# Hybrid decoder on one core: the rotated key rows written once a layer into four lasting K tiles, and two query squares added before their sums

## The chip, the cores and the metric

The kernel runs on one core of a Trainium2 chip. The metric is device time in microseconds (us), the median over several runs of the whole program. The engines of a core are named as the profile names them: PE is TensorE (matmuls and transposes), PEld its weight load, DVE is VectorE, ACT is ScalarE, POOL is GpSimd, and SP is SyncE, which issues the DMA transfers here.

## The reference

512 tokens with 1024 features go through two layers and a last RMSNorm. All is float32. Cut to what matters here:

```python
n = rmsnorm(h)
p = n @ W_in                      # RWKV groups, latents of the MLA, two gate groups
y_A = rwkv7_time_mix(p_A) @ W_oA  # 8 heads x 64; a group norm per head at the end
y_B = mla(p_B) @ W_oB             # 8 heads
h = h + (sigmoid(g_A) * y_A + sigmoid(g_B) * y_B) @ W_out
h = h + conv_ffn(rmsnorm(h))

def mla(q_lat, kv_lat, k_pe):     # widths 256, 128, 32
    q = rmsnorm(q_lat) @ w_q_up   # per head 64 plain + 32 rotary columns
    kv = rmsnorm(kv_lat) @ w_kv_up
    k_pe = rope(k_pe)             # one rotary key, the same for all 8 heads
    s = (q_nope @ k_nope + q_pe @ k_pe) * scale, causal
    return softmax(s) @ v
```

Two facts of it bear on the change: the rotated key rows are the same for all heads of a layer, and the RMSNorm of the query latent needs the sum of squares over 256 features, which the kernel holds as two tiles of 128 features.

## The kernel before

Tiles are 128 partitions x 512, features on the partitions and tokens along the row. A big matmul is done three times (L247 hi x hi, L248 lo x hi, L249 hi x lo), since each operand is split in two parts of lower precision. Weights come in units of 512 KB by DMA into `raw`; ACT makes the upper part `whi` (L202), DVE the lower part `wlo` (L203); there are two buffers of each. These matmuls are most of the program.

The stage around the change is the mixer of each layer. It runs in these steps.

1. **Inversion.** For the time mix, triangular 32x32 blocks are inverted on DVE: 30 dependent pairs of a product `tm` (L663) and an addition into `X` (L665), then the transposes `T11` (L667) and `T22` (L669), which the matmuls at L750 read. Meanwhile PE works on the weight units of the three latents (`lat`, two for q and one for kv, L689) and of the rotary key. The order of PE is written out by hand here (`tc.manual_schedule`). For each latent ACT makes the squares `lsq` (L693). `lsum` adds them over the features with `tok_sums` (L326): a matmul with one output column for each block of 128 tokens and each tile of squares, so 8 for the two query latents and 4 for the kv latent. DVE scales the sum (`nv`, L305), POOL takes the power -1/2 (L306), ACT spreads it (`nw`), and PE's transposes with a DVE step give `rq` (L319) and `rk`. Between them DVE computes the rotated key rows `kp` in three steps (L728 to L730) into the lower half (rows 64 to 127) of a tile. After that, DVE scales the kv latent (L736).
2. **Scan** over eight chunks, also in PE order by hand. POOL scales the state there (`tmp`, L815).
3. **Outputs, norms, heads.** `chunk_out` writes the output Y of the time mix into `Z`. `group_norm` and `group_scale` norm it for four blocks of tokens: DVE reduces (L856 to L860), POOL takes the power (L862) and scales (`Z`, L867). PE transposes the four normed blocks (L873, `xy<-cst,Z`). Beside this run the attention heads in four pairs, `heads(0)` to `heads(3)`. A pair has its plain key rows from PE, which ACT copies into K[0:64]; POOL copies `kp` into K[64:128] (L918); `q` is written by DVE (L925). Then come the scores `sc` (L933), the softmax in `P` on DVE (L936, L940) and ACT (L939, L941), the transposes `pt` (L944), their copies `PT` (L946) and the product `po` (L953), with the PE order by hand for L953 alone.

Outside of the parts ordered by hand a list scheduler sets the order of each engine when the program is built; it uses its own estimates of durations and the free buffers of each pool. K and q share five buffers (tag `qk`).

Of the kernel before, what the change touches and what calls it, by code (L numbers as in the profile page):

```python
# [9 lines left out]
F32 = mybir.dt.float32  # L10
# [3 lines left out]
ALU = mybir.AluOpType  # L14
# [144 lines left out]
def build(ctx, tc, x, pos, wst, vecd, constd, out):  # L159
    nc = tc.nc  # L160
    V, A, G, PE = nc.vector, nc.scalar, nc.gpsimd, nc.tensor

    def pool(**kw):
        return tc.tile_pool(reuse_waits="tile", **kw)
# [107 lines left out]
    def acc():  # L272
        return accp[-1].tile([128, 512], F32, name="acc", tag="acc")
# [19 lines left out]
    def rsqrt_tok(ps, n, eps, js=range(4), pool=sm, tag="nsq", bufs=1):  # L293

        v = rsqrt_col(ps, n, eps, js)
        w = pool.tile([128, 512], F32, name="nw", tag=tag, bufs=bufs)
        a, b = js[0], js[-1] + 1
        A.copy(w[:, 128 * a:128 * b].rearrange("p (j n) -> p j n", n=128),
               v[:, a:b, None].to_broadcast([128, b - a, 128]))
        return w  # L300
# [21 lines left out]
    def tok_sums(ps, sq, js=range(4)):  # L322
        sq = sq if isinstance(sq, list) else [sq]
        for j in js:
            for i, t in enumerate(sq):
                PE.matmul(ps[:, j:j + 1], t[:, 128 * j:128 * j + 128], ones[:, 0:1], start=i == 0, stop=i == len(sq) - 1)  # L326
# [100 lines left out]
    def mixer(l, ops, nrm, wks):  # L427
        with ExitStack() as mx:
# [209 lines left out]
            tl = mx.enter_context(pool(name=f"tl{l}", bufs=1))  # L638
# [3 lines left out]
            def sc(name="sc"):  # L642
                return pb.tile([128, 512], F32, name=name, tag="sc", bufs=2)
# [7 lines left out]
            with pool(name=f"ti{l}", bufs=2) as ti, tc.manual_schedule(engines={PE.engine}):  # L651
# [32 lines left out]
                lat, sq = [], []  # L684

                def lat_end(ps):
                    i = len(lat)
                    o = (tl if i < 3 else ti).tile([128, 512], F32, name=f"lat{i}", bufs=1)
                    V.tensor_tensor(o, ps, rstd, ALU.mult)  # L689
                    lat.append(o)  # L690
                    if i < 3:
                        sq.append(ti.tile([128, 512], F32, name="lsq", tag="lsq", bufs=3))
                        A.activation(sq[i], o, AF.Square)  # L693

                def a_ak_v(i):
                    ps = xyt()
                    for hd in range(8):
                        for e in range(2):
                            ur, vr = rows(e)
                            PE.matmul(ps[ur:ur + 64, e, 64 * hd:64 * hd + 64], AM[vr:vr + 64, hd, 2 * i + e, ur:ur + 64],  # L700
                                      Z[vr:vr + 64, i, e, 64 * hd:64 * hd + 64], start=True, stop=True, tile_position=(vr, ur))
                    for e in range(2):
                        ur, vr = rows(e)
                        A.copy(Z[ur:ur + 64, i, e, :], ps[ur:ur + 64, e, :])

                def lsum(i, t, n):
                    ssq = sc()
                    tok_sums(ssq, t)
                    return rsqrt_tok(ssq, n, NORM_EPS, pool=ti, tag="lsq", bufs=3)
# [9 lines left out]
                for i in range(3):  # L719
                    parts4[i].go()  # L720
                a_ak_v(0)
                w0 = lsum(0, sq[0:2], 256.0)
                parts4[3].go(4)
                w1 = lsum(1, sq[2], 128.0)
                parts4[3].go()
                kp = tl.tile([128, 512], F32, name="kp", bufs=1)
                k2 = ti.tile([128, 512], F32, name="k2", tag="lsq", bufs=3)
                V.tensor_tensor(kp[64:128, :], lat[3][0:64, :], tabs[0][0:64, :], ALU.mult)  # L728
                V.tensor_tensor(k2[64:128, :], lat[3][64:128, :], tabs[0][64:128, :], ALU.mult)
                V.tensor_tensor(kp[64:128, :], kp[64:128, :], k2[64:128, :], ALU.add)  # L730
                rq = tl.tile([128, 512], F32, name="rq", bufs=1)
                spread(w0, tabs[1], rq, sc)
                a_ak_v(1)
# [47 lines left out]
                for c in range(8):  # L781
                    i, e = divmod(c, 2)
# [38 lines left out]
            with pool(name=f"tb{l}", bufs=2) as tb:  # L821
                def MT(name, tag, bufs=3):
                    return tb.tile([128, 512], F32, name=name, tag=tag, bufs=bufs)
# [87 lines left out]
                def heads(p):  # L911
                    psk = acc()
                    mm3(psk, [w[:, 128 * p:128 * p + 128] for w in lk], kvop, True, True)
                    qs, ks = [], []
                    for hh in range(2):
                        K = MT("K", "qk", 5)
                        A.copy(K[0:64, :], psk[64 * hh:64 * hh + 64, :])
                        G.tensor_copy(K[64:128, :], kp[64:128, :])  # L918
                        ks.append(K)
                    for hh in range(2):  # L920
                        psq = acc()
                        for j in range(2):
                            mm3(psq, W.get(), qops[j], j == 0, j == 1)
                        q = MT("q", "qk", 5)
                        V.tensor_tensor(q, psq, rq, ALU.mult)  # L925
                        qs.append(q)
                    po = pb.tile([128, 512], F32, name="po", tag="po")
# [42 lines left out]
    for l in range(DEPTH):  # L970
# [7 lines left out]
        with pool(name=f"h{l + 1}", bufs=8, side="right") as hp, accs(f"accC{l}", 6):  # L978
# [31 lines left out]
            with pool(name=f"ff{l}", bufs=44) as fp:  # L1010
# [39 lines left out]
                if last:  # L1050
                    m = KT - 1
                    ws = [W.get() for _ in range(FT)]
                    with tc.manual_schedule(engines={PE.engine}):
                        for f in range(2):
# [10 lines left out]
                            sq = sm.tile([128, 512], F32, name="sq7", tag="nsq", bufs=1)  # L1065
# [47 lines left out]
```

## Time and profile before

| | |
|---|---|
| runs before | 1574.63 us median of 3 (1572.89 to 1576.72) |
| profiled execution, first to last instruction (span) | 1573.0 us |
| time around the span in the profiled execution | not given apart from the span; the runs' median is 1.6 us above it |
| instructions | 22441 |
| mean granted clock of PE over the span | 0.997 |
| L306, POOL power on 128x4 or 128x8, 10 times | 10.0 us in all, 998 ns each |
| L342, POOL addition of squares in the larger norms, 14 times | 25.0 us in all, 1787 ns each |
| L933, scores, 128 times | 44.4 us in all, 447 ns each |
| L203, DVE lower parts of weights, 249 times | 306.8 us in all, 1233 ns each |

The profile shows one execution. The busy time of an engine is the time in which its instructions run, with no register, branch or semaphore work. The chain of work is followed back from the last instruction: at each step to what released it. In the rows of the timeline the columns are start, duration, engine, line, operation, written tile and read tiles with their shapes; in brackets stand the idle time before the row and what ended it. Lines are those of the kernel before.

### The profile page before, as it was taken

The page shows a single profiled execution, that of the slowest core. Times are in us where ns is not written, and L with a number is a line of the kernel's source. Part 1 is how long each engine was busy: PE and PEld are TensorE (multiplying, and loading weights), DVE is VectorE, ACT ScalarE, POOL GpSimd, SP SyncE. Part 2 cuts the span into 40 slices and gives each one's busy share as a digit, 9 for nine tenths or more (in the row PEclk, how much of TensorE's full clock was granted, in tenths as well). Part 3 has the DMA queues.
Part 4 walks back from the last instruction along what each step waited for, and adds up shares of the span by engine and source line. Part 5 has one row for each costly group of instructions (what it writes and reads, how often), then busy time and mean ns, then how long its engine had stood idle before and what let it go on. Part 6 is the DMA issues. An engine that isn't in the chain of part 4 may idle for free.

```text
span 1573.0 us, 22441 instructions
## 1 busy us (share of the span) xinstructions
PE 1543.9 (98%) x9052; PEld 1248.4 (79%) x9052; DVE 917.0 (58%) x1476; ACT 664.0 (42%) x1004; POOL 184.4 (12%) x157
## 2 busy tenths in 40 slices
PE   8999999899999999999999999998999999999998
PEld 6887886678888888888878888776788888888887
DVE  6579786666555555533346768858574555554332
ACT  6445444663443333322244544447444433333222
POOL 1011102300310110100001110013002101100000
PEclk9999999999999999999999999999999999999999
DMA  6324322234323322233342333213353223222322
GB/s 207 115 94 144 118 82 68 82 94 148 121 94 95 102 98 94 94 113 119 110 147 93 109 107 121 75 49 103 100 168 101 94 95 104 97 94 94 102 99 81
DMA packets 57273, 166.09 MB, mean 106 GB/s; under 512 B 6352, under 2 KB 8528, under 8 KB 57168
## 3 DMA queue, kind: packets, MB, share of 16 engines
q1 hardware_dynamic: 57024, 164.48, 32.1%
q8 instruction: 71, 1.16, 0.3%
q14 instruction: 34, 0.28, 0.1%
q10 hardware_dynamic: 144, 0.16, 0.0%
HBM read 147.32 MB, written 17.30 MB: 105 GB/s over the span
## 4 chain that ended last, share of the span: by engine, by line
PE 90%; DVE 5%; ACT 2%; issue 1%; POOL 0%; DMA 0%; SPq 0%; POOLq 0%; DVEq 0%; ACTq 0%
PE acc L247 26%; PE acc L248 26%; PE acc L249 26%; PE sc L933 2%; PE pt L944 1%; PE po L953 1%; PE m L603 1%; PE xy L799 1%; DVE wlo L203 1%; PE m L611 1%; PE xy L808 0%; ACT whi L202 0%; DVE X L665 0%; DVE tm L663 0%; PE xy L789 0%
## 5 line engine op out<-in xcount | busy, mean ns | idle before, releaser
L247 PE MATMUL acc<-hi,whi 128*128 128x512 f32 (+1 forms) x1910 | 750.7, 393 | 6.0 <-ACT hi L283 5.1
L249 PE MATMUL acc<-hi,wlo 128*128 128x512 f32 (+1 forms) x1910 | 743.3, 389 | 1.7 <-issue 0.9
L248 PE MATMUL acc<-lo,whi 128*128 128x512 f32 (+1 forms) x1910 | 743.2, 389 | 0.0
L202 ACT CAST whi<-raw 128x1024 fp32r<-128x1024 f32 (+2 forms) x249 | 253.4, 1019 | 540.0 <-PE acc L248 466.6
L247 PEld LDWEIGHTS acc<-hi,whi 128*128 128x128 f32 x1910 | 359.6, 188 | 80.6 <-ACT hi L283 5.1
L249 PEld LDWEIGHTS acc<-hi,wlo 128*128 128x128 f32 x1910 | 359.5, 188 | 76.3 <-issue 1.7
L248 PEld LDWEIGHTS acc<-lo,whi 128*128 128x128 f32 x1910 | 359.8, 188 | 71.7 <-issue 0.8
L203 DVE TENSOR_TENSOR wlo<-raw,whi 128x1024 fp32r<-128x1024 f32 (+2 forms) x249 | 306.8, 1233 | 176.0 <-ACT whi L202 175.5
L1033 POOL TENSOR_TENSOR c<-c,rstd 128x512 f32<-128x512 f32 x44 | 58.0, 1317 | 403.5 <-ACT c L1032 403.5
L1026 DVE TENSOR_TENSOR u<-acc,rstd 128x512 f32<-128x512 f32 x44 | 30.5, 692 | 104.4 <-PE acc L249 104.3
L1035 DVE TENSOR_TENSOR c<-c,acc 128x512 f32<-128x512 f32 x44 | 30.3, 688 | 86.4 <-POOL c L1033 86.4
L1032 ACT ACTIVATE c<-c 128x512 f32<-128x512 f32 x44 | 27.8, 632 | 81.7 <-DVE c L1031 81.7
L306 POOL TENSOR_TENSOR nv<-nv,cst 128x4 f32<-128x4 f32 (+1 forms) x10 | 10.0, 998 | 337.2 <-DVE nv L305 335.9
L342 POOL TENSOR_TENSOR nacc<-nacc,nsq 128x512 f32<-128x512 f32 x14 | 25.0, 1787 | 193.7 <-ACT nsq L341 193.7
L933 PE MATMUL sc<-K,q 128*128 128x128 f32 (+3 forms) x128 | 44.4, 447 | 1.6 <-DVE q L925 1.6
L452 DVE TENSOR_TENSOR cur<-acc,rstd 128x512 f32<-128x512 f32 x28 | 19.1, 689 | 45.2 <-PE acc L249 37.7
L939 ACT ACTIVATE P<-P,mn 128x128 f32<-128x128 f32 (+3 forms) x64 | 35.5, 556 | 20.7 <-issue 9.3
L941 ACT ACTIVATE P<-P,mn 128x128 f32<-128x128 f32 (+3 forms) x64 | 34.4, 557 | 8.0 <-DVE mn L940 8.0
L1029 ACT ACTIVATE c<-u,vec 128x512 f32<-128x512 f32 x44 | 35.7, 811 | 2.8 <-DVE u L1025 2.8
L936 DVE CUSTOM_DVE_ANT_0 P<-sc,cst 128x128 f32<-128x128 f32 (+3 forms) x64 | 30.6, 483 | 5.9 <-PE xy L873 2.9
L1031 DVE SCALAR_TENSOR_TENSOR c<-u,vec,c 128x512 f32<-128x512 f32 x44 | 33.1, 752 | 1.5
L1030 DVE SCALAR_TENSOR_TENSOR c<-u,vec,c 128x512 f32<-128x512 f32 x44 | 32.8, 746 | 1.8 <-ACT c L1029 1.8
(247 smaller groups left out, 1356.7 us busy)
## 6 DMA issues: line engine op xcount, KB each, us to landing
raw<-in_w SPq DMA_DIRECT2D x238, 512.0 KB, 3.4
gate_d<-gg SPq DMA_DIRECT2D x32, 256.0 KB, 2.1
AM<-gate_d SPq DMA_DIRECT2D x16, 256.0 KB, 5.0
gb<-gate_d SPq DMA_DIRECT2D x16, 256.0 KB, 3.6
h<-in_x SPq DMA_DIRECT2D x8, 256.0 KB, 4.3
rgate_d<-gt SPq DMA_DIRECT2D x8, 256.0 KB, 2.6
bl_d<-rk SPq DMA_DIRECT2D x8, 256.0 KB, 4.4
bl<-bl_d SPq DMA_DIRECT2D x8, 256.0 KB, 2.6
```

Of the source, the lines that this page charges most:

```text
L202: A.copy(hi, r)
L203: V.tensor_tensor(lo, r, hi.bitcast(F32), ALU.subtract)
L247: PE.matmul(ps, w[0], xx[0], start=first, stop=False)
L248: PE.matmul(ps, w[0], xx[1], start=False, stop=False)
L249: PE.matmul(ps, w[1], xx[0], start=False, stop=last)
L933: PE.matmul(sp[:, 0:n], qs[hh][:, 128 * b:128 * b + 128], ks[hh][:, 0:n], start=True, stop=True)
L939: A.activation(P[:, 0:n], P[:, 0:n], AF.Exp, bias=mn[:, 0:1], scale=-1.0, accum_out=mn[:, 1:2])
L941: A.activation(P[:, 0:n], P[:, 0:n], AF.Copy, scale=mn[:, 2:3])
L1029: A.activation(cc, u[:, 2:514], AF.Identity, bias=vc(l, "conv_b", i), scale=vc(l, "conv_w", 2 * FT + i))
L1030: V.scalar_tensor_tensor(cc, u[:, 1:513], vc(l, "conv_w", FT + i), cc, ALU.mult, ALU.add)
L1031: V.scalar_tensor_tensor(cc, u[:, 0:512], vc(l, "conv_w", i), cc, ALU.mult, ALU.add)
L1033: G.tensor_tensor(cc, cc, rstd, ALU.mult)
```

## The change

Two parts. First, the squares of the two query latents are added on POOL into one tile as soon as both are there, so that `lsum(0, ...)` takes four one-column matmuls a layer in place of eight. Second, four tiles `K0` to `K3` of the mixer's lasting pool `tl` take the place of the eight K tiles of a layer's heads. DVE writes the rotated rows straight into `K0[64:128]`, POOL copies them into the other three right away, in the inversion, and `heads(p)` writes only rows 0 to 63 of the pair of tiles that is its turn (`K0`, `K1` for p = 0 and 2, `K2`, `K3` for p = 1 and 3). The q tiles have a tag of their own with three buffers. A layer has three POOL copies of the rotated rows in place of eight.

```diff
@@ lat_end(ps)
                         sq.append(ti.tile([128, 512], F32, name="lsq", tag="lsq", bufs=3))
                         A.activation(sq[i], o, AF.Square)
+                        if i == 1:
+                            G.tensor_tensor(sq[0], sq[0], sq[1], ALU.add)
...
                 a_ak_v(0)
-                w0 = lsum(0, sq[0:2], 256.0)
+                w0 = lsum(0, sq[0], 256.0)
                 parts4[3].go(4)
                 w1 = lsum(1, sq[2], 128.0)
                 parts4[3].go()
-                kp = tl.tile([128, 512], F32, name="kp", bufs=1)
+                Ks = [tl.tile([128, 512], F32, name=f"K{i}", bufs=1) for i in range(4)]
+                kp = Ks[0]
                 k2 = ti.tile([128, 512], F32, name="k2", tag="lsq", bufs=3)
                 V.tensor_tensor(kp[64:128, :], lat[3][0:64, :], tabs[0][0:64, :], ALU.mult)
                 V.tensor_tensor(k2[64:128, :], lat[3][64:128, :], tabs[0][64:128, :], ALU.mult)
                 V.tensor_tensor(kp[64:128, :], kp[64:128, :], k2[64:128, :], ALU.add)
+                for K in Ks[1:]:
+                    G.tensor_copy(K[64:128, :], kp[64:128, :])
                 rq = tl.tile([128, 512], F32, name="rq", bufs=1)
@@ heads(p)
-                    qs, ks = [], []
+                    qs, ks = [], Ks[2 * (p % 2):2 * (p % 2) + 2]
                     for hh in range(2):
-                        K = MT("K", "qk", 5)
-                        A.copy(K[0:64, :], psk[64 * hh:64 * hh + 64, :])
-                        G.tensor_copy(K[64:128, :], kp[64:128, :])
-                        ks.append(K)
+                        A.copy(ks[hh][0:64, :], psk[64 * hh:64 * hh + 64, :])
                     for hh in range(2):
                         psq = acc()
                         for j in range(2):
                             mm3(psq, W.get(), qops[j], j == 0, j == 1)
-                        q = MT("q", "qk", 5)
+                        q = MT("q", "q")
                         V.tensor_tensor(q, psq, rq, ALU.mult)
```

The lines behind the first added one move down by 2, those behind the key rows by 5, those behind the head's first loop by 2. Two places of the order that the scheduler and the program give show what moves.

POOL in layer 0, from ahead of the inversion through the scan to the first group norm, before (`whi` and `wlo` into `lk`: weights of the keys; `St`, `PC`: the scan's state and decay; `mu`: the group norm's statistics):

```order
L579 TENSOR_TENSOR BKb<-BK,z 128x1024
L306 TENSOR_TENSOR nv<-nv,cst 128x4 x2
L815 TENSOR_TENSOR tmp<-St,PC 128x256 x3
L901 CAST lk_2584<-whi 128x512
L901 CAST lk_2586<-wlo 128x512
L918 COPY K<-kp 64x512
L815 TENSOR_TENSOR tmp<-St,PC 128x256
L918 COPY K<-kp 64x512 x2
L815 TENSOR_TENSOR tmp<-St,PC 128x256 x2
L918 COPY K<-kp 64x512
L862 TENSOR_TENSOR mu<-mu,cst 128x8
```

The same stretch of POOL after:

```order
L579 TENSOR_TENSOR BKb<-BK,z 128x1024
L695 TENSOR_TENSOR lsq<-lsq 128x512
L306 TENSOR_TENSOR nv<-nv,cst 128x4 x2
L735 COPY K_1966<-K_1965 64x512
L735 COPY K_1967<-K_1965 64x512
L735 COPY K_1968<-K_1965 64x512
L820 TENSOR_TENSOR tmp<-St,PC 128x256 x3
L906 CAST lk_2587<-whi 128x512
L906 CAST lk_2589<-wlo 128x512
L820 TENSOR_TENSOR tmp<-St,PC 128x256 x3
L867 TENSOR_TENSOR mu<-mu,cst 128x8
```

An addition of 128x512 and three copies of 64x512 now stand in the inversion, where POOL had only the two small powers; the four copies during the scan are gone.

PE in layer 0, around the third of the group norm's transposes (`xy<-cst,Z`), before; `acc` are the queries of a later head:

```order
L933 MATMUL sc<-K,q 128x128
L247 MATMUL acc<-hi,lk_2584 128x512
L248 MATMUL acc<-lo,lk_2584 128x512
L873 MATMUL xy<-cst,Z 128x128 x2
L249 MATMUL acc<-hi,lk_2586 128x512
L933 MATMUL sc<-K,q 128x128
L247 MATMUL acc<-hi,whi 128x512
L933 MATMUL sc<-K,q 128x256
L873 MATMUL xy<-cst,Z 128x128
L248 MATMUL acc<-lo,whi 128x512
```

The same place of PE after:

```order
L935 MATMUL sc<-K_1967,q 128x128
L247 MATMUL acc<-hi,lk_2587 128x512
L248 MATMUL acc<-lo,lk_2587 128x512
L878 MATMUL xy<-cst,Z 128x128 x2
L249 MATMUL acc<-hi,lk_2589 128x512
L878 MATMUL xy<-cst,Z 128x128
L935 MATMUL sc<-K_1968,q 128x128
L247 MATMUL acc<-hi,whi 128x512
L935 MATMUL sc<-K_1967,q 128x256
L248 MATMUL acc<-lo,whi 128x512
```

The third transpose now stands ahead of a score, a weight matmul and a longer score that stood ahead of it; the fourth comes after the rest of the query's matmuls and a score of 384 columns, where before it came after two scores of 512. In layer 1 the same pieces move.

## The prediction

> **What bounds the kernel now.** The page comes first: the busy shares and the chain of work that ended last.
>
> ```profile
> span 1573.0 us, 22441 instructions
> PE 1543.9 (98%) x9052; PEld 1248.4 (79%) x9052; DVE 917.0 (58%) x1476; ACT 664.0 (42%) x1004; POOL 184.4 (12%) x157
> PE 90%; DVE 5%; ACT 2%; issue 1%; POOL 0%; DMA 0%; SPq 0%; POOLq 0%; DVEq 0%; ACTq 0%
> ```
>
> TensorE is busy for 98% and carries 90% of the chain, so a change counts only where TensorE idles, or by taking work from it while nothing else is late. Next comes the table of busy time by stretch (columns: stretch, length, then the busy time of PE, PEld, DVE, ACT and POOL, the granted clock, the DMA share, GB/s). The first row is the triangular inversion of layer 0, the two below it are the group norms of layers 0 and 1, and the last is the rest of layer 0's attention heads.
>
> ```profile
> 190.00:223.00 33.00, 33.00 (x268) 27.36 (x268) 30.64 (x77) 13.10 (x19) 2.26 (x2) 1.00 0.25 79
> 283.00:307.00 24.00, 19.95 (x271) 13.77 (x270) 17.05 (x48) 14.08 (x35) 12.61 (x11) 0.93 0.32 111
> 1060.00:1084.00 24.00, 20.08 (x280) 14.06 (x280) 18.18 (x52) 15.50 (x37) 12.61 (x11) 1.00 0.34 111
> 307.00:345.00 38.00, 37.80 (x259) 26.57 (x259) 28.41 (x84) 29.99 (x74) 0.61 (x1) 1.00 0.22 66
> ```
>
> Two places matter. In the inversion PE is busy all the time, but DVE is too (30.64 of 33.00 us; what is left are gaps of 0.03 between dependent steps, and two waits). In the group norms PE idles 4.05 and 3.92 us. Behind them it idles 0.20 us, so PE is the bound again there, and what is lost before stays lost.
>
> **The inversion: which engine ends last.** The timeline's columns are start, duration, engine, line, operation; in brackets the idle time before it and its releaser.
>
> ```profile
> 196.80 0.63 ACT L693 ACTIVATE lsq<-lat 128x512 f32<-128x512 f32 x1 [1.38 <-DVE lat L689]
> 200.96 1.95 PE L326 MATMUL sc<-cst,lsq 128*128 128x1 f32 x16
> 205.61 0.95 PE L326 MATMUL sc<-cst,lsq 128*128 128x1 f32 x8
> 205.58 0.41 DVE L665 TENSOR_TENSOR X<-X,tm 128x240 f32<-128x240 f32 x1
> 206.60 0.16 DVE L305 TENSOR_SCALAR nv<-sc 128x4 f32<-128x4 f32 x1 [0.61 <-PE sc L326]
> 209.44 0.69 DVE L689 TENSOR_TENSOR lat<-acc,rstd 128x512 f32<-128x512 f32 x1 [0.19 <-PE acc L249]
> 223.16 2.19 DVE L667 STREAM_TRANSPOSE T<-X 128x1024 f32<-128x1024 f32 x1
> 225.40 2.21 PE L750 MATMUL sc<-T,AM 32*32 32x32 f32 x128 [0.35 <-DVE T L667]
> ```
>
> DVE's chain of tm and X ends in the transpose T; PE stands waiting for it (0.35 us). So DVE sets the end of this stage.
>
> *The sums.* Four of eight one-column matmuls go (8 records of 16): 1.95 - 0.95 = 1.0 us of PE. PE comes 1.0 us earlier to a wait that DVE ends, so by itself this is worth nothing. What it does free is DVE's two waits on PE: 0.61 and 0.19, less the usual gap of 0.03 each, so 0.74 us a layer.
>
> *The added addition and the three copies* stand on POOL, which is empty there. The squares that the addition reads are there at 197.43, its sums begin at 200.96, and the copies were made at 254.0 us at the earliest before (last row below), so by their own duration they cost nothing. The question is what they do to DVE. No row has POOL at work beside the tm and X chain on tiles of this size; the nearest rows are these.
>
> ```profile
> 80.83 1.92 POOL L579 TENSOR_TENSOR BKb<-BK,z 128x1024 f32<-128x1024 f32 x1 [7.21 <-DVE BK L573]
> 80.73 0.69 DVE L588 TENSOR_TENSOR rk<-m,v 128x512 f32<-128x512 f32 x1
> 81.34 2.48 DVE L203 TENSOR_TENSOR wlo<-raw,whi 128x1024 fp32r<-128x1024 f32 x1
> 84.75 1.21 DVE L203 TENSOR_TENSOR wlo<-raw,whi 128x1024 fp32r<-128x1024 f32 x1
> 398.43 2.05 DVE L203 TENSOR_TENSOR wlo<-raw,whi 128x1024 fp32r<-128x1024 f32 x1 [0.20 <-ACT whi L202]
> 400.15 1.49 POOL L342 TENSOR_TENSOR nacc<-nacc,nsq 128x512 f32<-128x512 f32 x1 [0.74 <-ACT nsq L341]
> 400.41 1.78 DVE L284 SCALAR_TENSOR_TENSOR lo<-h,vec,hi 128x512 fp32r<-128x512 f32 x1
> L918 POOL COPY K<-kp x16: 609/613/617, 254.0 to 1094.4; 64x512 f32<-64x512 f32 x16
> ```
>
> L203 takes 1.21 us alone and 2.48 beside POOL: POOL ends at 82.75, L203 at 83.82, 1.07 later, as if it had only begun when POOL was done. L588, one of whose inputs lies in PSUM, was not slowed (0.69). At 400.15 POOL waits for L203 (ends at 400.48), then works 1.16 us until 401.64, and L284 takes 1.78, where the same form takes 0.75 undisturbed (lat at 214.61, below). So a DVE step with both inputs in SBUF and a POOL step that reads SBUF exclude each other. The steps tm and X have both inputs in SBUF. The addition has the shape of L342, so it takes 1.16 us of DVE's chain (bounds: 0, and 1.49, the whole row). The copies take 0.61 each: 0 to 1.83 us. What DVE does behind the last kp step:
>
> ```profile
> 213.45 0.38 DVE L665 TENSOR_TENSOR X<-X,tm 128x210 f32<-128x210 f32 x1
> 213.74 0.69 DVE L319 TENSOR_TENSOR rq<-sc,tab 128x512 f32<-128x512 f32 x1
> 214.34 0.36 DVE L663 TENSOR_TENSOR tm<-X 128x198 f32<-128x198 f32 x1
> 214.61 0.75 DVE L736 SCALAR_TENSOR_TENSOR lat<-lat,vec,rk 128x512 f32<-128x512 f32 x1
> ```
>
> X starts first; the first copy then runs beside rq, which reads PSUM, and costs nothing. The second and third fall on tm, lat and the next X: 2 x 0.6 = 1.2 us, which I take. Sum for the stage: +1.16 + 1.2 - 0.74 = +1.6 us a layer (bounds -0.7 and 1.49 + 1.83 - 0.74 = +2.6). T comes 1.6 later and PE waits 0.35 + 1.0 + 1.6 = 3.0 us for it. Two layers: **+3.2 us**.
>
> **The heads.** The eight copies of kp that go from each layer are priced at nothing: none of them stands ahead of a wait of PE, and POOL is empty around them. The new buffers (four K and three q, in place of five in common) let a later head start earlier, and the scheduler uses this: ahead of the group norm's third transpose (L873, xy<-cst,Z) stood three pieces of head work, which now stand behind it. Before:
>
> ```profile
> 293.80:296.89 3.09, 1.16 (x6) 0.71 (x5) 3.04 (x13) 2.56 (x9) 2.68 (x2) 1.00 0.01 3
> 294.58 0.49 PE L933 MATMUL sc<-K,q 128*128 128x128 f32 x2 [0.78 <-DVE q L925]
> 294.82 0.48 PE L247 MATMUL acc<-hi,whi 128*128 128x512 f32 x1
> 295.14 0.59 PE L933 MATMUL sc<-K,q 128*128 128x256 f32 x2
> 295.80 1.04 POOL L867 TENSOR_TENSOR Z<-Z,mu 128x512 f32<-128x512 f32 x1
> 296.89 0.46 PE L873 MATMUL xy<-cst,Z 128*128 128x128 f32 x1 [1.16 <-POOL Z L867]
> 295.45 0.27 DVE L936 CUSTOM_DVE_ANT_0 P<-sc,cst 128x128 f32<-128x128 f32 x1
> 297.84 0.67 DVE L860 TENSOR_REDUCE mu<-Z 128x8 f32<-128x512 f32 x1
> 301.48 1.04 POOL L867 TENSOR_TENSOR Z<-Z,mu 128x512 f32<-128x512 f32 x1
> 305.30 0.66 PE L953 MATMUL po<-PT,Vt 128*64 128x128 f32 x8 [0.48 <-ACT PT L946]
> ```
>
> POOL's third Z comes no earlier (nothing in its chain is changed), so PE now stands the whole 3.09 us from 293.80 to 296.89 in place of 1.93: +1.16. The second score, pushed behind 296.89, reaches DVE at about 297.4 rather than 295.45. Queued behind it there are the next P, L203 and the reduction of the fourth norm: 297.4 + 0.27 + 0.42 + 1.22 + 0.67, then a copy and a small step, 300.6. POOL's power (1.64) and Z (1.04) follow, about 303.5 rather than 302.52. The fourth transpose stands earlier in PE's order than it did: PE's rows ahead of it sum to some 5.1 us, so it is there at 302.0 and waits 1.5 us. The later wait for PT (0.48) should go, since the PT copies are ready then. Idle time: 1.16 + 1.5 - 0.48 = +2.2 us a layer.
>
> The clock comes on top.
>
> ```profile
> 293.54:296.95 3.41, 1.48 (x8) 0.77 (x7) 3.36 (x13) 2.88 (x9) 2.68 (x2) 1.00 0.01 2
> 296.95:300.37 3.42, 3.42 (x9) 2.33 (x10) 2.39 (x8) 0.94 (x4) 0.61 (x1) 0.50 0.38 123
> 1071.70:1075.12 3.42, 2.05 (x10) 1.49 (x11) 3.37 (x11) 2.40 (x9) 2.39 (x2) 1.00 0.03 7
> ```
>
> In layer 0 a stretch of 3.41 us with 1.48 busy was followed by one of 3.42 at half clock, in which PE was busy throughout: 1.7 us lost. In layer 1 a stretch with 2.05 busy was not. With 3.09 us idle in one piece, both layers should now fall under the limit. Half clock there doubles one short score, one L247 and one longer score ahead of the fourth norm, about +0.9; the rest falls into the 1.5 us of waiting. Layer 0: 2.2 + 0.9 - 1.7 = +1.4. Layer 1: 2.2 + 0.9 = +3.1. Heads together **+4.5 us**. Bounds: 0, if the waits are filled, and 3.1 x 2 = 6.2, if layer 0 would have paid its half clock anyway.
>
> The Trainium skill (TensorE: Matmul & The Clock Gate, section "What's actually happening") has the half clock come after an idle window of some 3.4 us; the row above shows it after a window 43% busy, so the measurement decides. By the page neither layer would pay, and the sum would be 1.8 us lower, as in rival 4.
>
> Sum: 3.2 + 4.5 = +7.7 us on the profiled 1573.0. The runs' median is 1574.63 (1572.89 to 1576.72), so I add it there: 1582.3, said as 1582.
>
> **Rivals.** (1) *No exclusion*: the POOL steps find the gaps, DVE's chain loses nothing and the freed waits remain: 2 x -0.74 + 4.5 = +3.0, 1577.6. For it: the steps of the chain are 0.2 to 0.4 us long, with gaps. Against: 0.03 us is no room for a step of 0.6 us, and POOL won the wait at 400.48.
> (2) *The heads catch up*: waits move but do not grow, since the same norms end them and PE saturates behind: +3.2 alone, 1577.8. For it: PE idles only 0.20 us after 307. Against: that is why lost time cannot be won back there.
> (3) *The heads gain*: more buffers let PE fill its idle time with work of a later head. Place: the waits at the third transpose and PT, 1.93 + 0.48 and about as much in layer 1. Price: all of them, -4.7, with the freed waits -1.5: 1568.4. It decides once the third transpose finds head work ahead of it. Against: in the order it has less of it ahead than before.
> (4) *No half clock*, if PE's work on both sides of the 3.09 us keeps the clock up: heads 2.2 + 2.2 - 1.7 = +2.7, with the stage's 3.2 1580.5. For it: the stretch with 2.05 busy. Against: the one with 1.48, busier than what is left now.
>
> **Chances.** Main case 0.52 (1579 to 1587), no exclusion 0.17, heads catch up 0.11, no half clock 0.13, heads gain 0.07. A change of under 0.2% (3.15 us) can hardly be told from none here. Rivals 1 and 2 lie at that bound and share out: slower 0.74, same 0.19, faster 0.07. For the range: the low end takes in rivals 1 and 2 with the runs' own spread (1575.5). The high end has the copies at their full 1.83 (+1.2 for both layers), the addition at 1.49 (+0.7), heads at 6.2 (+1.7) and one half-clock stretch begun by the 3.0 us wait for T (up to +1.7); not all at once, so 1587.
>
> **What would show it.** In the changed trace: tm, X or lat steps of 0.9 to 1.5 us beside POOL's addition and copies; no wait ahead of nv at L305; a wait of 2 to 3 us of PE for T; 3 us of PE idle ahead of the third transpose and over 1 us ahead of the fourth; a half-clock stretch in both layers' norms. The prediction is wrong if tm and X keep their durations beside POOL, or if PE's idle time in the norms stays at 4 us.

## The result, and the profile after

The changed kernel is slower. Beside the kernel before, 6 runs of each gave 1583.99 us median (1580.41 to 1589.30) against 1575.10 (1572.89 to 1578.53): ratio 1.0060, 95% interval 1.0044 to 1.0076, which is +9.5 us (here and below a difference in us is what the ratio makes of the median before). A second time, on another occasion, it was 1580.76 us (7 runs, 1579.99 to 1583.79) against 1574.98 (24 runs): ratio 1.0037, interval 1.0024 to 1.0050, +5.8 us. The two are 3.7 us apart; both intervals hold a difference of 7.7 us. The prediction was 1582: 7.7 us added to 1574.63, the median of the runs before.

The page of the changed kernel shows almost nothing of it: span, busy time and the chain by engine.

```profile
span 1579.4 us, 22381 instructions
PE 1544.5 (98%) x9036; PEld 1248.7 (79%) x9036; DVE 918.0 (58%) x1476; ACT 666.1 (42%) x1004; POOL 182.6 (12%) x149
PE 90%; DVE 5%; ACT 2%; issue 2%; POOL 1%; DMA 0%; SPq 0%; POOLq 0%; DVEq 0%; ACTq 0%
```

PE's busy time is up by 0.6 us and the span by 6.4. The difference is in waits, and in matmuls at half clock that count as busy. So the time was taken apart by stages, each from one event to the next: I from the start of X's first transpose (L659) to the first matmul that reads T; S (the scan and the outputs) from there to the first pair of the norm's transposes; H from there to the next layer's L659, or to the end of the span. H holds the heads and all that follows. In us, layer 0 and layer 1, from the first and last rows of each stage in the profiled execution:

| kernel | I0 | I1 | S0 | S1 | H0 | H1 |
|---|---|---|---|---|---|---|
| before | 37.94 | 37.94 | 67.76 | 68.95 | 670.44 | 502.51 |
| changed | 38.66 | 38.58 | 67.68 | 67.74 | 671.74 | 505.85 |
| changed, again | 38.67 | 38.66 | 68.69 | 68.66 | 670.89 | 504.58 |
| squares alone | 38.17 | 38.03 | 68.69 | 74.51 | 668.81 | 502.53 |
| K tiles alone | 38.56 | 40.14 | 67.73 | 68.67 | 671.44 | 505.89 |
| K copies on ACT | 37.99 | 37.96 | 68.66 | 68.66 | 671.84 | 505.33 |
| addition on DVE, copies on ACT | 37.56 | 37.58 | 67.75 | 67.74 | 671.61 | 505.37 |
| nine K copies | 40.53 | 40.52 | 74.47 | 70.06 | 670.91 | 505.52 |
| changed, fourth ahead of third | 38.58 | 38.61 | 68.67 | 68.70 | 670.63 | 506.20 |
| before, fourth ahead of third | 37.94 | 37.94 | 67.76 | 71.86 | 668.80 | 502.57 |
| the same, again | 39.53 | 37.95 | 67.78 | 68.39 | 668.82 | 502.65 |
| before, transposes behind the third pair | 37.93 | 37.94 | 67.79 | 71.86 | 668.63 | 502.24 |
| before, own buffers for K and q | 37.93 | 37.94 | 67.78 | 68.82 | 672.74 | 503.18 |
| changed, wait for T filled | 38.73 | 38.73 | 73.25 | 68.81 | 670.79 | 504.30 |

What comes ahead of I0 took 1.69 us more in the changed kernel's profiled execution, by a half-clock stretch at 22.7 us in code that the change doesn't touch. It isn't counted below. The other 4.7 us are I (+0.72 and +0.64), S (-0.08 and -1.21), H0 (+1.30) and H1 (+3.34). In the second profiled execution of the changed kernel the same six differences are +0.73, +0.72, +0.93, -0.29, +0.45 and +2.07, 4.6 us in all.

The -1.21 of S1 is a gain that the prediction doesn't have. In the kernel before, PE stands in layer 1's scan ahead of one matmul of a weight unit, and the profile names nothing that ended the wait ("issue"):

```profile
1009.61 0.50 PE L249 MATMUL acc<-hi,wlo 128*128 128x512 f32 x1 [0.93 <-issue]
```

This wait is there in all five profiles of the kernel before and of its versions in experiments 5, 6 and 8 (0.93 us, in one of them 0.38), and in none of the other nine, the two parts alone included. What it is, no run shows.

**The inversion.** Rows of the changed kernel's timeline: the addition and the X step beside it, the second sum, the copies with the steps beside them, and PE's wait for T.

```profile
198.57 1.22 DVE L203 TENSOR_TENSOR wlo<-raw,whi 128x1024 fp32r<-128x1024 f32 x1
199.13 1.81 POOL L695 TENSOR_TENSOR lsq<-lsq 128x512 f32<-128x512 f32 x1 [23.10 <-ACT lsq L693]
199.70 1.46 DVE L665 TENSOR_TENSOR X<-X,tm 128x198 f32<-128x198 f32 x1
208.62 0.15 DVE L305 TENSOR_SCALAR nv<-sc 128x4 f32<-128x4 f32 x1
215.34 2.00 POOL L735 COPY K<-K 64x512 f32<-64x512 f32 x3 [5.33 <-DVE K L733]
215.53 0.68 DVE L319 TENSOR_TENSOR rq<-sc,tab 128x512 f32<-128x512 f32 x1
216.13 0.73 DVE L663 TENSOR_TENSOR tm<-X 128x198 f32<-128x198 f32 x1
216.78 1.10 DVE L741 SCALAR_TENSOR_TENSOR lat<-lat,vec,rk 128x512 f32<-128x512 f32 x1
227.81 2.21 PE L755 MATMUL sc<-T,AM 32*32 32x32 f32 x128 [2.03 <-DVE T L667]
```

POOL waits until L203 is done (199.79), works 1.15 us to 200.94, and the X step, 0.36 before, ends 0.22 after it: 1.10 lost. The wait of 0.61 ahead of nv is gone. Beside the copies rq, which reads PSUM, keeps its 0.68; tm takes 0.73 instead of 0.36 and lat 1.10 instead of 0.75: 0.72 lost. The three together are 1.10 + 0.72 - 0.74 = 1.08; T is 0.82 later behind L659 (the 0.26 between them was not traced), and PE, which is 1.0 earlier, waits 2.03 us instead of 0.35.

**The norms.** PE at the third and the fourth transpose and at PT, with POOL's Z, layer 0; then the same two transposes in layer 1.

```profile
298.06 1.04 POOL L872 TENSOR_TENSOR Z<-Z,mu 128x512 f32<-128x512 f32 x1
299.16 0.45 PE L878 MATMUL xy<-cst,Z 128*128 128x128 f32 x1 [3.02 <-POOL Z L872]
299.40 0.64 PE L935 MATMUL sc<-K,q 128*128 128x128 f32 x2
306.69 0.33 PE L878 MATMUL xy<-cst,Z 128*128 128x128 f32 x1 [0.66 <-POOL Z L872]
313.23 0.88 PE L955 MATMUL po<-PT,Vt 128*64 128x128 f32 x12 [0.18 <-DVE PT L948]
1077.22 0.33 PE L878 MATMUL xy<-cst,Z 128*128 128x128 f32 x1 [3.02 <-POOL Z L872]
1084.61 0.33 PE L878 MATMUL xy<-cst,Z 128*128 128x128 f32 x1 [0.50 <-POOL Z L872]
```

The three pieces that stood ahead of the third transpose are behind it, so that PE stands 3.02 us in one piece. In the 65 us from the first pair on PE idles 0.61 + 3.02 + 0.66 + 0.18 = 4.47 us, where before it was 0.60 + 0.78 + 1.16 + 0.48 = 3.02. In layer 1 it is 4.31 against 2.89. In the second profiled execution there is no wait at the fourth transpose in either layer, and the idle time is 3.80 and 3.81 us.

**The clock** behind these waits, in the table by stretch (columns as in the prediction's): in each layer a stretch in which PE is busy 0.39 us, and then one at half clock.

```profile
295.81:299.22 3.41, 0.39 (x3) 0.07 (x3) 2.09 (x8) 2.86 (x7) 2.68 (x2) 1.00 0.00 1
299.22:302.63 3.41, 3.41 (x10) 2.84 (x11) 1.58 (x5) 1.10 (x4) 0.00 (x0) 0.50 0.00 0
1074.06:1077.47 3.41, 0.39 (x3) 0.25 (x3) 1.91 (x8) 2.67 (x7) 2.68 (x2) 1.00 0.00 0
1077.28:1080.69 3.41, 3.41 (x10) 2.71 (x11) 1.72 (x5) 1.09 (x4) 0.00 (x0) 0.53 0.00 0
```

So H0 grows by 1.4 us of idle time (it had a half-clock stretch before as well), and H1 by 1.4 of idle time and by a new stretch.

### The profile page after: what moved, and what is told of

Its sections match the earlier page's. It is cut to its first block, busy times and chain, and to the rows that moved or that the text cites. A ratio compares the mean times of both kernels' runs of the same rounds, so it can differ in the third digit from the quotient of the medians.

```text
span 1579.4 us, 22381 instructions
## 1 busy us (share of the span) xinstructions
PE 1544.5 (98%) x9036; PEld 1248.7 (79%) x9036; DVE 918.0 (58%) x1476; ACT 666.1 (42%) x1004; POOL 182.6 (12%) x149
## 3 DMA queue, kind: packets, MB, share of 16 engines
q8 instruction: 71, 1.16, 0.3%
## 4 chain that ended last, share of the span: by engine, by line
PE 90%; DVE 5%; ACT 2%; issue 2%; POOL 1%; DMA 0%; SPq 0%; POOLq 0%; DVEq 0%; ACTq 0%
PE acc L247 26%; PE acc L249 26%; PE acc L248 26%; PE sc L935 2%; PE pt L946 1%; PE po L955 1%; PE m L603 1%; PE xy L804 1%; DVE wlo L203 1%; PE m L611 1%; ACT whi L202 1%; PE xy L813 0%; POOL mu L867 0%; DVE tm L663 0%; PE xy L794 0%
## 5 line engine op out<-in xcount | busy, mean ns | idle before, releaser
L203 DVE TENSOR_TENSOR wlo<-raw,whi 128x1024 fp32r<-128x1024 f32 (+2 forms) x249 | 305.6, 1229 | 175.5 <-ACT whi L202 175.1
```

The lines of the kernel that those rows point to most:

```text
L203: V.tensor_tensor(lo, r, hi.bitcast(F32), ALU.subtract)
```

## The experiments

**1. The two parts apart.** The squares' addition alone:

```diff
 # the kernel before
+                        if i == 1:
+                            G.tensor_tensor(sq[0], sq[0], sq[1], ALU.add)
...
-                w0 = lsum(0, sq[0:2], 256.0)
+                w0 = lsum(0, sq[0], 256.0)
```

> The addition of the two query squares alone; K copies, buffers and PE's order in the heads as before. Theory (the POOL addition and DVE's steps on X exclude each other): one X step beside the addition takes about 1.46 us instead of 0.36 as in the trace after (+1.1), the waits of 0.61 and 0.19 go (-0.74), so T comes 0.4 us later after X's first transpose, PE's wait for T is 0.35 + 1.0 + 0.4 = 1.7 us a layer, and the time is +0.7 us against before. Norms as before, 4.0 us idle a layer. Rival (no exclusion, the gain of the freed waits remains): -1.5 us, wait for T of 0.6 us. Second rival (the whole +9 us comes from the sums' part): +9 us.

Measured: 1575.38 us (12 runs, 1571.97 to 1583.22) against 1574.98, ratio 1.0009 (0.9992 to 1.0025): +1.4 us, not told from none. The X step is that of the theory, so the first rival (no exclusion) is out; rows of its timeline:

```profile
197.81 1.81 POOL L695 TENSOR_TENSOR lsq<-lsq 128x512 f32<-128x512 f32 x1 [23.09 <-ACT lsq L693]
198.38 1.46 DVE L665 TENSOR_TENSOR X<-X,tm 128x198 f32<-128x198 f32 x1
```

The inversion grows by 0.23 and 0.09, PE waits 1.48 and 1.34 us for T (1.7 expected), and H0 and H1 are those of the kernel before without a half-clock stretch (668.81, 502.53). What the theory had not counted is the clock behind the wait for T, further below. The second rival, that the sums carry all of the loss, is out.

The K tiles alone (the changed kernel without the edits just shown):

> The four lasting K tiles alone; the sums are before's eight one-column matmuls. Theory: the three POOL copies cost DVE's chain 0.7 us a layer (tm 0.73 for 0.36, lat 1.10 for 0.75), the waits of 0.61 and 0.19 stay, T comes 0.7 later; in the norms PE idles 3.0 ahead of the third transpose and about 0.6 ahead of the fourth, with half clock behind: +1.2 and +2.1 us. Sum +1.4 + 3.3 = +4.7 us, more if further half-clock stretches fall into the run. Rival (the heads are no worse, all of it is the inversion): +1.4 us. Rival (the squares' addition carries the loss): 0.

Measured: 1581.74 us (9 runs, 1580.28 to 1584.68), ratio 1.0038 (1.0026 to 1.0049): +6.0 us. H0 and H1 are the changed kernel's (671.44, 505.89), the third transpose waits 3.02 us again, and I0 is +0.62. Both rivals are out: the K tiles carry most of the loss, and most of that lies in the heads. (I1 has 1.6 us more by a half-clock stretch of its own, of which the last section tells.)

**2. The copies on ACT.**

```diff
 # the changed kernel
-                    G.tensor_copy(K[64:128, :], kp[64:128, :])
+                    A.copy(K[64:128, :], kp[64:128, :])
```

> The changed kernel with its three copies on ACT instead of POOL. Theory (copies cost only by POOL's exclusion with DVE): tm and lat behind rq are back at 0.36 and 0.75, T comes 0.7 earlier a layer than in the changed kernel; the norms lose the same: -1.4 us against the changed kernel, about +4.2 against before by the profile of one execution. Rival (the copies cost through their place, whoever makes them, or ACT's later whi holds PE): no better than the changed kernel, with waits of PE or DVE for ACT.

Measured: 1578.80 us (11 runs, 1577.65 to 1582.63), ratio 1.0018 (1.0008 to 1.0029): +2.8 us. DVE's steps behind the last key row, with ACT copying from 214.66 to 216.32:

```profile
214.95 0.68 DVE L319 TENSOR_TENSOR rq<-sc,tab 128x512 f32<-128x512 f32 x1
215.55 0.36 DVE L663 TENSOR_TENSOR tm<-X 128x198 f32<-128x198 f32 x1
215.82 0.75 DVE L741 SCALAR_TENSOR_TENSOR lat<-lat,vec,rk 128x512 f32<-128x512 f32 x1
```

tm and lat are back at 0.36 and 0.75. I is 0.67 and 0.62 shorter than in the changed kernel. The same copies at the same place cost DVE nothing when ACT makes them; the rival is out.

**3. The addition on DVE itself, the copies on ACT.**

```diff
 # the changed kernel
-                            G.tensor_tensor(sq[0], sq[0], sq[1], ALU.add)
+                            V.tensor_tensor(sq[0], sq[0], sq[1], ALU.add)
...
-                    G.tensor_copy(K[64:128, :], kp[64:128, :])
+                    A.copy(K[64:128, :], kp[64:128, :])
```

> The changed kernel with the squares added on DVE instead of POOL, and its three copies made by ACT. X's first transpose to T took 35.70 us before, 36.52 in the changed kernel, 35.82 with the copies on ACT alone. Theory (a POOL step on such tiles takes DVE's time for its own whole duration, 1.10 us were lost in the trace): DVE's own addition of 128x512 takes 0.69, so it is cheaper for DVE to add itself: 35.82 - 1.10 + 0.69 = 35.4 us; PE then waits about 1.0 us for T. The heads lose as in the changed kernel. Against the changed kernel -2.2 us in the two layers, against before about +3 to +4 by the medians. Rival (the X step was late for another reason, such as the squares coming late): 35.8 or more, and a DVE step beside it as slow as before.

Measured: 1577.05 us (11 runs, 1576.32 to 1578.48) against 1575.46, ratio 1.0011 (1.0002 to 1.0021): +1.7 us, where +3 to +4 were expected. The X step, the addition, and both ends of the chain in its timeline:

```profile
187.39 2.10 DVE L659 STREAM_TRANSPOSE X<-DX 128x1024 f32<-128x1024 f32 x1 [0.81 <-ACT DX L658]
197.94 0.36 DVE L665 TENSOR_TENSOR X<-X,tm 128x198 f32<-128x198 f32 x1
198.22 0.68 DVE L695 TENSOR_TENSOR lsq<-lsq 128x512 f32<-128x512 f32 x1
222.75 2.15 DVE L667 STREAM_TRANSPOSE T<-X 128x1024 f32<-128x1024 f32 x1
```

From L659 to T are 35.36 us, as the theory had it (35.4); 35.70 before, 36.52 in the changed kernel. The addition costs the busiest engine 0.68 us if that engine makes it, and 1.10 if POOL does it "beside" it. The heads still lose: H1 is 505.37.

**4. Nine copies instead of three**, in the kernel with the K tiles alone:

```diff
-                for K in Ks[1:]:
+                for K in Ks[1:] + Ks[1:] + Ks[1:]:
                     G.tensor_copy(K[64:128, :], kp[64:128, :])
```

> The lasting K tiles alone (sums as before), with each of the three POOL copies made three times, nine in all; the six more write the same rows again. X to T took 36.36 us with three copies, 35.70 before. Theory (each copy takes its own 0.61 us from DVE's chain once no DVE step that reads PSUM covers it): + 6 x 0.61 = 3.7, so 40.0 us a layer, with DVE's tm, X, lat and wlo steps each longer by up to 0.6. Rival (what costs is the beginning of POOL's work, or a fixed loss for one stretch): 36.4 to 36.7. Rival (they slow DVE by a share of the overlap, as the three did, 0.66 for 1.83): +1.3, 37.7 us.

Measured, in one profiled run (1591.09 us, with 17 us at half clock at the scan's start): from L659 to T are 38.49 us, 2.13 more than with three (layer 1: 38.50). All three expectations missed: the six more copies cost 0.36 us each, neither their whole 0.61 nor the 0.22 of the first three. POOL, and some of the DVE steps beside it:

```profile
213.32 7.27 POOL L733 COPY K<-K 64x512 f32<-64x512 f32 x9 [5.61 <-DVE K L731]
215.78 0.77 DVE L665 TENSOR_TENSOR X<-X,tm 128x198 f32<-128x198 f32 x1
216.47 1.63 DVE L203 TENSOR_TENSOR wlo<-raw,whi 128x1024 fp32r<-128x1024 f32 x1
218.02 0.75 DVE L663 TENSOR_TENSOR tm<-X 128x184 f32<-128x184 f32 x1
220.81 0.32 DVE L663 TENSOR_TENSOR tm<-X 128x150 f32<-128x150 f32 x1
```

Each DVE step with two SBUF inputs beside a copy loses 0.3 to 0.4 us once, whatever its length (X 0.77 for 0.36, L203 1.63 for 1.22), and a copy takes 0.81 on average instead of 0.61. By these rows they take turns, and a turn of the copy blocks DVE for only some 0.36 of its 0.61.

**5. The order at the third transpose.** In the changed kernel, and in the kernel before:

```diff
-                    for i in range(4):
-                        PE.transpose(ps[:, 128 * i:128 * i + 128], ...)
+                    tr(0)                # tr(i): the same transpose of block i
+                    tr(1)
+                    with tc.manual_schedule(engines={PE.engine}):
+                        tr(3)
+                        tr(2)
```

> The changed kernel, but PE's fourth transpose of the normed blocks is written ahead of the third, so that the third doesn't stand ahead of the heads' scores; the inversion keeps the addition and the copies. Theory (the heads' loss is PE waiting at the third transpose and the half clock behind it): idle in the norms falls from 5.3 to about 2 us a layer or less, no half clock there, and what is left is the inversion's +0.7 a layer: against the changed kernel -5 to -7 us, against before -2 to +1. Rival (other work of the heads is late then, or the order is not the cause): +4 us or more against before, with the same idle time at other tiles.

Measured in the changed kernel: 1581.27 us (11 runs, 1578.57 to 1585.94), ratio 1.0034 (1.0023 to 1.0046): +5.4 us, so the theory missed and the rival holds. PE's waits in the norms and heads of layer 0, behind the first pair:

```profile
296.78 0.49 PE L941 MATMUL sc<-K,q 128*128 128x128 f32 x2 [0.77 <-DVE q L933]
303.82 0.33 PE L878 MATMUL xy<-cst,Z 128*128 128x128 f32 x1 [1.36 <-POOL Z L872]
325.66 0.52 PE L952 MATMUL pt<-cst,P 128*128 128x128 f32 x3 [0.34 <-DVE mn L948]
326.84 0.88 PE L961 MATMUL po<-PT,Vt 128*64 128x128 f32 x12 [0.65 <-DVE PT L954]
329.27 1.13 PE L941 MATMUL sc<-K,q 128*128 128x256 f32 x4 [0.51 <-DVE mn L944]
```

No half clock follows in the norms, but 4.24 us are idle all the same (with the 0.61 ahead of the first pair): 1.36 at the transpose that now comes last, and later in the softmax of the last heads. In layer 1 it is 4.58 us, and there a half-clock stretch (1105.79 to 1109.20) follows waits of 1.19 at pt and 0.65 at po; H1 is 506.20, no less than the changed kernel's.

> The kernel before, with PE's fourth transpose of the normed blocks written ahead of the third; nothing of the change in it. Theory (waits at the transposes are lost time unless the heads only wait elsewhere later): the third's 1.16 us go in each layer, and with them layer 0's half-clock stretch of 1.7: -2 to -4 us. Rival, from the run with the same edit in the changed kernel (the time moved to waits for the last heads' softmax): no gain, 0 to +1 us, with waits of PE at pt and po.

Measured in the kernel before: 1573.79 us (12 runs, 1572.54 to 1577.55), ratio 0.9991 (0.9981 to 1.0001): -1.4 us. Again PE idles what it did (2.99 us against 3.02); the third transpose's wait is now one for the softmax:

```profile
299.22 0.33 PE L950 MATMUL pt<-cst,P 128*128 128x128 f32 x1 [1.25 <-ACT P L947]
```

So the waits are the rival's, and the time lies between the rival's and the theory's. The half-clock stretch of H0 is gone (668.80 against 670.44). That the new order takes it away isn't shown: with the squares alone layer 0 had before's order and waits, and no such stretch either (668.81).

The transposes emitted behind the third pair of heads, in the kernel before:

```diff
-for f in (outputs, norms, lambda: heads(0), lambda: heads(1), transposed, lambda: heads(2), lambda: heads(3)):
+for f in (outputs, norms, lambda: heads(0), lambda: heads(1), lambda: heads(2), transposed, lambda: heads(3)):
```

> The kernel before, with the group of the normed blocks' transposes emitted behind the third pair of heads instead of the second, so that the scheduler gives the heads precedence: the third transpose stands behind 8 more pieces of head work. Theory: PE's waits in the norms fall from 4 to about 2 us a layer and nothing else waits: -2 to -4 us. Rival (the two last pairs lack filler at their end, since the transposes and the next units come later): +1 to +4 us, with waits at pt and po.

Measured: 1575.39 us (12 runs, 1572.11 to 1577.70), ratio 0.9998 (0.9986 to 1.0011): no difference, so the theory missed. Idle in H0's first part: 2.99 us, with 1.14 at pt and 0.47 at po. In these three the waits moved and their sum stayed about what it was. Whether another order would have work for PE there, no run shows.

**6. Which part of the K tiles moves the order.** The kernel before with buffers of its own for K and for q:

```diff
-                        K = MT("K", "qk", 5)
+                        K = MT("K", "K", 4)
...
-                        q = MT("q", "qk", 5)
+                        q = MT("q", "q")
```

> The kernel before with tags of their own for K (four buffers) and q (three) as in the change, but with before's copy of the key rows for each head and before's sums. The scheduler then leaves the third transpose behind the three pieces of head work, as before, and puts the fourth ahead, as in the changed kernel. Theory (the heads' loss is the third transpose's wait of 3.0 us and the half clock behind it): third wait 1.2 us and q's wait 0.8 as before, at the fourth up to 0.5 us more; from the first transposes of layer 1 to the end 502.5 to 503.2 us (502.51 before, 505.85 in the changed kernel); against before 0 to +1.5 us. Rival (the buffers of their own are what costs, by what the heads do early): 505 us and more from there, +4 us or more against before.

Measured: 1577.18 us (11 runs, 1574.57 to 1578.67) against 1575.67, ratio 1.0007 (0.9998 to 1.0017): +1.1 us. In layer 1 the waits are 0.78, 1.15, 0.44, 0.18 and 0.20, H1 is 503.18: the theory's numbers. So the buffers alone cost 0.67 us there, at the fourth transpose and behind; the other 2.67 of H1's 3.34 come, by this difference, with the third transpose's early place and the clock behind it, which the buffers alone did not bring. What else of the K tiles moves it, the copies that are gone from the heads or the tiles that last, no run takes apart. Layer 0 shows something else (H0 672.74, and a wait of 2.57 us at the third transpose where 1.2 was expected):

```profile
296.54 2.08 POOL L867 TENSOR_TENSOR Z<-Z,mu 128x512 f32<-128x512 f32 x1
296.50 1.22 DVE L203 TENSOR_TENSOR wlo<-raw,whi 128x1024 fp32r<-128x1024 f32 x1
298.67 0.47 PE L873 MATMUL xy<-cst,Z 128*128 128x128 f32 x1 [2.57 <-POOL Z L867]
```

Here DVE began 0.04 us ahead of POOL, so POOL's Z waited for L203: 2.08 instead of 1.04, and PE with it. In the kernel before POOL was first at that place and L203 took 1.80. Half clock for 6.83 us (297.31 to 304.14) followed, so that the expected time came out with a layer 0 that wasn't expected.

**7. The changed kernel again, and with the wait for T filled.**

> The changed kernel once more, nothing edited, as the base of the next run and for another profile. Expected +9 us against before as first measured; the profile should again have T 36.5 us behind X's first transpose, waits of 2.0 us for T and 3.0 us at the third transpose. Open: its first runs reached from 1580.4 to 1589.3 us. Theory (the wait for T lets the clock fall to half at the scan's start in some runs, for one stretch of 3.4 us or several): runs with a mean clock of 0.988 to 0.993 are the long ones, and a profile of such a run has the stretches there. Rival: the long runs wait longer somewhere at a full clock.

Its time stands above: +5.8 us, not +9. The profiled run was the shortest of these runs (1579.99 us), so it doesn't show what the longest lose. It had the clock at half behind the wait for T in both layers, which the first profile had not; layer 0's stretch ahead and the stretch itself:

```profile
225.22:228.63 3.41, 1.91 (x119) 1.91 (x121) 3.41 (x3) 0.53 (x2) 0.00 (x0) 1.00 0.02 5
228.63:232.04 3.41, 3.41 (x33) 2.31 (x27) 3.29 (x6) 3.37 (x4) 0.00 (x0) 0.50 0.00 0
```

It costs 1.0 us a layer (S 68.69 and 68.66 against 67.68 and 67.74). In the run with the squares alone layer 1 had 17.08 us of half clock there, and S1 took 74.51. The first runs of 1586 to 1589 us had mean clocks of 0.988 to 0.990, where the profiled one of 1581.20 had 0.996; that they lost it at this place is likely by this, but no profile of one of them exists.

```diff
 # the changed kernel, ahead of L755
+                    for _ in range(0 if b else 16):
+                        PE.transpose(ps[:, 0:128], ident, ident)
```

> The changed kernel with 16 transposes of a constant, whose result is overwritten, written into PE's order right ahead of the first matmul that reads T (some 1.8 us of PE, in each layer, in the wait of 2.0 us). DVE's chain and T's time are the same, no useful work is added. Theory (half clock behind the wait for T costs extra in part of the runs): no half-clock stretch at the scan's start, the longest runs go, and the median is 2 to 4 us below the changed kernel run beside it. Rival (the length of the wait is all there is): within 0.5 us of the changed kernel. Rival (the clock falls there because the scan's own matmuls are small): the same spread as before.

Measured: 1582.46 us (6 runs, 1580.65 to 1585.52), ratio 1.0046 (1.0031 to 1.0062): no better. The test is not clean: with the 16 transposes the scheduler put a wlo step (L203, 1.19 us) ahead of the copies of Q, and PE, which now waited 0.35 us for T, waited 1.14 for Q. In layer 0 the clock fell there, for 10.25 us:

```profile
230.12:233.53 3.41, 2.07 (x92) 1.59 (x92) 2.78 (x5) 3.35 (x5) 0.00 (x0) 1.00 0.64 222
233.53:243.78 10.25, 10.25 (x96) 7.88 (x90) 2.30 (x4) 0.93 (x2) 0.00 (x0) 0.50 0.02 6
```

So the theory that the wait for T alone brings the half clock isn't shown. The kernel before with the fourth transpose first had half clock for 6.82 us from 1007.60 on, with a wait for T of only 0.35 us; it began behind 2.6 us of 32x32 matmuls, in the wait of 0.93.

**8. The version that came out ahead, once more**: the kernel before with the fourth transpose ahead of the third.

> The kernel before with the fourth transpose ahead of the third, once more, as the version that the runs so far point to (ratio 0.9991, interval 0.9981 to 1.0001). Theory (it gains only by layer 0's half-clock stretch, since its wait moved to the softmax of the next block: 1.25 us at pt): -1 to -2 us again. Rival (no difference): 0, within 0.5 us.

Measured: 1573.90 us (11 runs, 1572.75 to 1577.51) against 1575.46, ratio 0.9992 (0.9983 to 1.0001). Of the two times -1.4 and -1.3 us, both intervals just reach 1: it beats the changed kernel, and is not shown to beat the one before.

## Why the prediction was right, point by point

- *The addition on POOL* (+1.16 a layer): right; 1.10 lost by one X step, in two kernels, and none when DVE makes the addition itself, in 0.68 (experiments 1 and 3).
- *The copies* (+1.2 a layer): right in kind, too large. tm and lat lost 0.72, and I fell by 0.67 and 0.62 without them. The mis-sized step is "2 x 0.6": a copy blocks DVE for about 0.36 of its 0.61 us (experiment 4). The forecast took the exclusion from an addition, whose two inputs block for nearly the whole time, and carried it to a copy.
- *The freed waits* (-0.74): both gone. With these the inversion's sum was +1.6 a layer; it measured 0.72 and 0.64, and PE's wait for T 2.03 where 3.0 stood.
- *The third transpose* (3.09 us in one piece, +1.16): right, 3.02 in both profiles. The early place in the order comes with it: with before's place it was 1.15 in layer 1 (experiment 6). But with that wait taken away layer 1's heads lost as much elsewhere (H1 506.20 in experiment 5), so this one place isn't shown to be all of the heads' loss.
- *The fourth* (+1.5, at 303.5 us): too large: 0.66 and 0.50 in the first profile, nothing in the second. The PT wait fell from 0.48 to 0.18 instead of to nothing. Idle time grew by 1.45 and 1.42 (0.78 and 0.92 in the second profile) instead of 2.2.
- *Half clock in both norms*: right in both profiled runs. Of 14 profiled passages with a wait of 3.02 us at the third transpose 13 had it, of 13 in which no transpose waited over 1.4 us one (layer 0 of the kernel before); the one between them, 2.57 us in experiment 6, had it too. Layer 1's heads were forecast at +3.1 and measured +3.34, layer 0's +1.4 and +1.30. That these come so near is luck: in layer 1 the idle time was 1.4 instead of 2.2, and what the clock added 1.9 (3.34 less 1.42) instead of 0.9. In the second profile the heads lost +2.07 and +0.45.
- *The sum*: +7.7 forecast, +9.5 and +5.8 measured, but 4.7 and 4.6 in the stages of the two profiled executions. The inversion (1.4 instead of 3.2) and the idle time in the norms were taken too large, and the wait of S1 that goes was left out. Half clock behind the wait for T (1.0 in each layer in which it falls) stood only in the range's high end. Both profiled executions belong to the shorter ones of their runs, so the medians hold more than they show. The longest runs have lower mean clocks (0.988 to 0.990), which speaks for more half clock; where it falls, no profile shows. Apart from S1 the mechanisms are those that were forecast; that the number comes between the two medians is in part luck.
- *The rivals*: no exclusion, out by the X step of 1.46 us and by experiments 2 and 3; the heads catch up, out by H1; the heads gain, out: of the waits that it wanted filled, experiment 5 shows that they move to the softmax; no half clock, out in 13 of 14 passages.

The Trainium skill (SBUF — State Buffer, section "SBUF: two separate sides") says that of DVE with two SBUF inputs and POOL reading SBUF the one that starts first has the shared ports for its whole instruction, and the other waits. For the addition (1.10 of 1.15 us) and for Z behind L203 (2.08 for 1.04) the traces agree; for the copies (0.36 of 0.61) they don't.

## What to carry to other kernels

Work that is moved to an idle POOL beside a DVE chain of two-input SBUF steps is not hidden: the addition cost DVE 1.10 us from POOL and 0.68 on DVE itself, and the copies cost nothing on ACT. Where a list scheduler sets the order, an edit that takes away only work that cost nothing can move a wait ahead of useful work; compare the two orders around every wait of the bounding engine before looking at durations. A wait that was taken away there came back elsewhere: in the three kernels of experiment 5 PE idled 2.9 to 4.6 us a layer, about as much as without the edit, whichever instruction waited.

## What the runs showed of the hardware

*Half clock without idling.* In two profiled runs with the eight one-column sums the clock fell right behind them, though PE was busy all through the stretch ahead; one of them, stretch ahead and stretch itself, with the matmuls of the first:

```profile
199.60:203.02 3.42, 3.42 (x51) 3.06 (x50) 3.25 (x9) 1.56 (x2) 0.00 (x0) 0.99 0.32 123
202.95:206.36 3.41, 3.41 (x9) 2.64 (x9) 2.96 (x7) 1.96 (x4) 1.16 (x1) 0.50 0.39 132
199.90 1.15 PE L700 MATMUL xy<-Z,AM 64*64 64x64 f32 x32
200.98 1.95 PE L326 MATMUL sc<-cst,lsq 128*128 128x1 f32 x16
```

It cost that inversion 1.6 us (I0 39.53 against 37.94 in the second run of before's kernel with the fourth transpose first; I1 40.14 against I0's 38.56 with the K tiles alone). With eight sums it fell there in 2 of 14 passages, with four in none of 14. A matmul with one column, or on 32x32 or 64x64 tiles, is busy in the profile and seems to count little for the clock: the stretches at the scan's beginning also lie behind such matmuls. The counts are small, and no run here changed the matmuls' shapes alone.

*The stretches are multiples.* Apart from those that run into the end of the program, 3.41, 6.83, 10.25 and 17.08 us were measured, 1, 2, 3 and 5 times 3.41, in part at other places in two runs of the same kernel. The Trainium skill (TensorE: Matmul & The Clock Gate, section "What's actually happening") has the clock set by windows of some 3.4 us that don't start with the kernel, and the half clock come after an idle window. The lengths agree with that; the stretch ahead that was busy throughout doesn't.

*The exclusion goes to whoever is first*, by 0.04 us in experiment 6, and the loser can be the one on the critical path.
